# One decoder layer on one core: query and key loads of the prompt's heads on SyncE's queue, the samples' recurrence traced in two pieces

## The chip, the core and the metric

The kernel runs on one core of a Trainium2 chip. The metric is the device time of one execution in microseconds (us). Work on an engine is issued in the order of that engine's queue: PE (TensorE), DVE (VectorE), ACT (ScalarE), POOL (GpSimd) and SP (SyncE, which only issues transfers and waits). Sixteen DMA engines move the data of all queues.

## The reference

The kernel computes one layer for 1024 prompt tokens and, beside them, 8 sample sequences of 8 tokens each. The mixing part has two halves of 512 channels: a recurrent one (8 heads of 64 channels, a matrix state per head) and an attention one (8 heads, three dilated windows, a distance bias). Both feed one output projection, and a mixture of experts follows. The two parts that the change touches are these:

```python
def wkv_scan(s0, r, decay, k, v, kk, a):
    def step(s, inp):
        r_t, w_t, k_t, v_t, kk_t, a_t = inp
        s_kk = jnp.einsum('bhvk,bhk->bhv', s, kk_t)
        s = (s * w_t[:, :, None, :]
             - s_kk[..., None] * (kk_t * a_t)[:, :, None, :]
             + v_t[..., None] * k_t[:, :, None, :])
        return s, jnp.einsum('bhvk,bhk->bhv', s, r_t)
...
    scores = jnp.einsum('brnqhd,brnkhd->brnhqk', qb, kb) * (HEAD_DIM ** -0.5)
...
    o = jnp.einsum('brnhqk,brnkhd->brnqhd', e, vb) / jnp.swapaxes(den, -1, -2)[..., None]
```

The first is the recurrence; here it is the samples' that matters (8 sequences, 8 tokens, states from the cache). The second is the prompt's attention.

## The kernel before

Phase 1 normalizes the tokens, projects them (L264) and writes what later stages need to DRAM: among it the prompt's queries QP and keys KP, channel-major, each as an exact sum of two parts (a tensor of [2, 512, 1024]). Phase 2 runs the prompt's recurrence in chunks. Phase 3 is the attention, phases 4 to 6 are the output projection, the experts and the end.

**Attention of the prompt.** `phase3` (from L994) walks over pairs of heads; a pair has two heads, and a head has query tiles of 128 rows, ia to ib of 8. It is called twice: in the first call, while phase 2 still ends, heads 0 and 1 do tiles 0 to 4 (L936); in the second (L946) heads 0 and 1 do tiles 5 to 7, and pairs 1, 2 and 3 do all eight. For each tile PE multiplies queries with keys (L1040, two matmuls per 512 keys), DVE adds the bias and takes the maximum (L1043), ACT exponentiates (L1052), PE turns the result (L1063) and multiplies with the values (L1069), DVE scales (L1070).

**A head's operands** come from `head` (L963): keys `k` over both parts (128 rows: 64 channels of the high part, then 64 of the low part), queries `q` twice, once per part, each with its 64 rows given to both halves of the partitions, and the bias table. Each has two buffers, so a head's loads can start when the head two before it has done its last L1040. `head` is called for the head at work and for the next one. Its key and query loads are issued on POOL's queue (L971, L974), the bias on SP's (L976). Their source is a pattern written out by hand:

```python
        dup = lambda x, r, step, a, b: bass.AP(tensor=x.tensor, offset=x[0, r:r + 1, a:a + 1].offset, ap=[[step, 2], [NP, 64], [1, b - a]])
```

The outermost dimension of that source has two entries, and 64 rows lie in each. Another load of the kernel, on SP's queue, has a source of the same make: `At` in `solve` (L680), for the chunk systems of phase 2, 32 rows per load, with four entries outermost:

```python
                                  bass.AP(tensor=src.tensor, offset=src.offset, ap=[[0, 4], [1024, 8], [1, 1024]]))
```

**The samples' recurrence** is `phase2s` (L583), between the two calls of `phase3`. `prepA` and `prepB` make its operands, `solve_s` (L728) writes the 8 x 8 systems to DRAM (ABs, L620), reads them back one per partition (A8, L737), inverts them on DVE (L742, L744), writes them (XZ, L750) and reads them as TTs (L752). `sample2` (L792) then goes over four pairs of heads: it loads the cached states (s0s, L802), needs TTs in its matmul L820, and writes the new states (L844). `epilogue` (from L846) finishes the samples' rows. All PSUM of this part is one bank.

**Order.** The order of instructions on each engine is made at build time by a planner, which takes the traced order as priority and places an instruction when its operands and buffers are free by its own model of time. So where a piece is traced decides how early it stands in each queue. SP is in order too: behind an instruction that waits, all later loads of that queue wait. A hook of `phase3` runs just before a pair is traced: at pair 2 the samples' tiles are given up and w_out is loaded and split (`then`, L942). During pairs 1 and 2 twelve copies of the cache, 1016 KB each from DRAM to DRAM, are issued on SP (L281), each after an exponential.

Of the kernel before, what the change touches and what calls it, by code (L numbers as in the profile page):

```python
# [10 lines left out]
F32 = mybir.dt.float32  # L11
F32R = mybir.dt.float32r
F16 = mybir.dt.float16
# [8 lines left out]
NP = 1024  # L22
# [7 lines left out]
XB = 4      # tiles of x in flight  # L30
# [3 lines left out]
class K:  # L34
# [9 lines left out]
    def split(self, hi, lo, src, lo_eng=None, hi_eng=None):  # L44
        """hi + lo == src exactly; hi and lo carry float32r values."""
        nc = self.nc
        (hi_eng or nc.scalar).activation(hi, src, AF.Copy) if (hi_eng or nc.scalar) is nc.scalar else hi_eng.tensor_copy(hi, src)  # L47
        e = lo_eng or nc.vector
        return e.tensor_tensor(lo, src, hi.bitcast(F32), op=ALU.subtract)  # L49

    def bcast_row(self, vec, n):
        """DRAM vector of n values as [128, n], the same on each partition."""
        return bass.AP(tensor=vec.tensor, offset=vec.offset, ap=[[0, 128], [1, n]])

    def rstd(self, pool, ss, n, width, eps, scale, tag):
        """(ss*scale + eps)^-0.5 for a [n, width] tile."""
        nc = self.nc
        ms = pool.tile([128, width], F32, tag=tag + "m", name=tag + "m")
        nc.vector.tensor_scalar(ms[:n], ss, scale, eps, op0=ALU.mult, op1=ALU.add)
        r = pool.tile([128, width], F32, tag=tag + "r", name=tag + "r")  # L60
        nc.gpsimd.tensor_tensor(r[:n], ms[:n], self.mhalf[:n, :width], op=ALU.pow)  # L61
        return r
# [10 lines left out]
    def dram(self):  # L73
        d = self.es.enter_context(self.pool("dram", space=DRAM))
        self.dp = d
        t = lambda n, s, dt=F32: d.tile(s, dt, name=n)
        self.XV = t("XV", [4, 128, T])           # value, per pair of heads, channel-major
        self.ARd = t("ARd", [4, 128, 17, 128])   # per chunk: removal key | receptance, times the decay so far; last chunk: samples
        self.KB = t("KB", [4, 128, T])           # key over the decay so far
        self.BB = t("BB", [4, 128, T])           # removal key times a over the decay so far  # L80
        self.PC = t("PC", [4, 128, 24])          # decay over a chunk; 16 prompt chunks, 8 sequences
        self.BV = t("BV", [4, 128, T])           # bonus
        self.AA = t("AA", [4, 128, T])
        self.GG = t("GG", [4, 128, T])
        self.SS = t("SS", [T, 512])
        self.QP = t("QP", [2, 512, NP])          # prompt queries, channel-major, as an exact sum of two float32r parts
        self.KP = t("KP", [2, 512, NP])
        self.QT = t("QT", [4, 128, NS])
        self.KT = t("KT", [4, 128, NS])
        self.VS = t("VS", [NS, 512])  # L90
        self.KS = t("KS", [NS, 512])

# [1 line left out]
    def phase1(self):  # L94
        nc, tc, I, O = self.nc, self.tc, self.I, self.O
        with ExitStack() as es:
# [13 lines left out]
            # projection, 25 tiles of 128 columns, the lora tile first; the first two go along with the norm  # L110
# [33 lines left out]
            # last projected rows  # L144
# [7 lines left out]
    def vectors(self, c1):  # L152
        nc, I = self.nc, self.I
        nc.sync.dma_start(self.cst, I['cst'])
        # per-channel vectors, channel-major
# [23 lines left out]
        # mu * state_shift, [128, b, ct]  # L179
# [68 lines left out]
    def project(self, ct, out, chunks=range(3)):  # L248
        """columns 128 ct.. of the projection, channel-major; those of RWKV shifted by a token"""
# [28 lines left out]
    def copy(self, c, after):  # L278
        """Half of a sample's cache moves on, not before another instruction; the last rows come with the projection."""
# [33 lines left out]
    def lora(self, lora, lp):  # L313
        nc, I, vec, pm = self.nc, self.I, self.vec, self.pm1
        # contractions over 32 or 64 rows: the data's high and low parts stacked, the weights' parts in two passes
# [47 lines left out]
    def rwkv_ops(self, p, xr, xk, xv, ep):  # L363
        """per-token operands of a pair of heads: decay products within chunks, keys, bonus"""
# [7 lines left out]
        # decay so far within the chunk: before and after the token  # L372
# [17 lines left out]
        # removal key, normalized per head, negated  # L390
# [12 lines left out]
        # key  # L403
# [3 lines left out]
        # bonus  # L407
# [11 lines left out]
        # products with the decay  # L419
# [23 lines left out]
def host_consts():  # L443
    """Tables that depend on shapes alone."""
# [10 lines left out]
    # identity rows for a quarter of the columns: column 4c + d on partitions with (p // 8) % 4 == d  # L455
# [5 lines left out]
class K2(K):  # L461
# [17 lines left out]
    def pools2c(self, es):  # L479
        """tiles that stay over the RWKV stage and the samples' part of it"""  # L480
        nc = self.nc
        self.c2 = c2 = es.enter_context(self.pool("c2", side="right"))
        # zero-padded block-diagonal operands; the padding is written once
# [27 lines left out]
    def pools2a(self, es):  # L511
        """the first of pools2, opened while the projection still runs"""
# [28 lines left out]
    def phase2a(self):  # L541
        """the first chunks' systems, which the projection hides"""
# [40 lines left out]
    def phase2s(self):  # L583
        y = self.e2.tile([128, 512], F32, tag="y", name="y")
        G = self.prepA('s')
        self.prepB('s', G)
        self.solve_s(G)
        self.sample2(G, y)
        self.epilogue(NP, y, 64)

    def pair_load(self, dst, src, t0, nck):
        """[pair, channel, token] into the block-diagonal [channel, chunk, pair, (head, token)]"""
# [5 lines left out]
    def prepA(self, u):  # L598
        """what the chunk systems and the states' first products need; two chunks, or the samples"""
# [71 lines left out]
    def solve(self, u, G):  # L671
        """(I - A)^-1 of each 64 x 64 chunk system: 32-row halves by forward substitution, joined by products.
        Partition (head of the pair, half, column mod 4, chunk and pair)."""
# [19 lines left out]
    def join(self, u, G):  # L693
        nc, sv, X = self.nc, self.sv, G['X']
        TT = G['TT'] = self.TT[u % 2]
        R1 = sv.tile([128, 8, 32], F32, tag="R1", name="R1")     # rows: [t, column / 4, (column mod 4, system)]
        RT = sv.tile([128, 8, 32], F32, tag="RT", name="RT")     # transposed: [column, system, t]
# [3 lines left out]
        # diagonal halves; systems of pairs 0, 1 on rows 0..63, of pairs 2, 3 on rows 64..127  # L701
# [26 lines left out]
    def solve_s(self, G):  # L728
        """inverse of the 8 x 8 systems, one per partition (pair, head, sequence)"""
# [62 lines left out]
    def sample2(self, G, y):  # L792
# [4 lines left out]
        for p in range(4):  # L797
            # states, rows (sequence parity, v), then turned to [(head, k), (sequence, v)]
# [28 lines left out]
            for j, (src, lhs) in enumerate(((G['Vt'][:, 0, p, :], G['Kt']), (u, G['Bt']))):  # L827
                # rows spread over their sequence
# [69 lines left out]
class K3(K2):  # L898
# [3 lines left out]
    def attn_out(self, pool, X, at, n, i0, gat, tags=("asq", "an", "ao"), bufs=1, w=512):  # L902
        """rmsnorm of [n, 512] mixed heads, then channel-major into MX[4:8]."""
# [19 lines left out]
    def phase123(self):  # L923
# [5 lines left out]
        with ExitStack() as ea:  # L929
# [16 lines left out]
            self.phase3([(0, 5, 8), (1, 0, 8), (2, 0, 8), (3, 0, 8)], 3, (3, 2, 1, 1), {AHEAD: then})  # L946
# [16 lines left out]
    def head(self, h, ia, ib):  # L963
        """a head's operands for query tiles ia..ib"""
# [4 lines left out]
        # keys: high over low part; queries: either part twice  # L969
        k = self.qk.tile([128, NP], F32R, tag="k", name="k3")  # L970
        nc.gpsimd.dma_start(k[:, :w], dup(self.KP, h * 64, 512 * NP, 0, w))  # L971
        q = self.qk.tile([128, 2, NP], F32R, tag="q", name="q3")
        for a in range(2):
            nc.gpsimd.dma_start(q[:, a, 128 * ia:w], dup(self.QP[a:a + 1], h * 64, 0, 128 * ia, w))  # L974
# [4 lines left out]
    def samples_out(self, pool, X, n, w):  # L979
        """the samples' heads, from rows per head to rows per token"""  # L980
# [13 lines left out]
    def phase3(self, pairs, depth, banks, hooks={}):  # L994
        nc, tc, I, O = self.nc, self.tc, self.I, self.O
        gat, at = self.gat, self.at
        with ExitStack() as es:
# [5 lines left out]
            else:       # stays for the following phases  # L1003
# [154 lines left out]
ORD = (8, 0, 1, 2, 3, 4, 5, 6, 7)     # of the token tiles in phase 4, and of their routing tables  # L1158
# [16 lines left out]
class K4(K3):  # L1175
# [8 lines left out]
    def ahead(self):  # L1184
        """w_out, loaded and split while the attention still runs"""
# [34 lines left out]
    def pst(self, tag):  # L1220
        """a bank of PSUM, from the rings of the attention"""
# [8 lines left out]
    def hold(self, d, after):  # L1230
        """a load that waits for an instruction"""
# [3 lines left out]
    def load_w(self, j, after=(None, None), part=(0, 1)):  # L1235
        """block j: -2, -1 w_out; 0..31 the experts' gate | up; 32, 33 w_ple_gate"""
# [13 lines left out]
    def split_w(self, j, q, eng=None, after=None):  # L1250
        """quarter q of block j"""
# [8 lines left out]
    def load_d(self, j, after=None):  # L1260
        """block j: 0..31 the experts' down; 32 w_ple; 33 p of the prompt"""
# [16 lines left out]
    def mm3(self, p, a, b, k0, k1, kn, c=slice(0, 512)):  # L1278
        """p += a^T b over chunks k0..k1 of kn, in three float32r passes"""
# [11 lines left out]
    def phase4_(self, p4):  # L1291
# [19 lines left out]
        ones = p4.tile([128, 128], F16, name="ones")      # counts and token numbers are exact in float16  # L1311
# [43 lines left out]
        def logits(i, last=False):  # L1355
            """of the router; the norm's gain is in its weights, its scale comes last"""
# [18 lines left out]
        def route(i0, nb):  # L1375
            """experts, weights and slots of nb token tiles"""
# [4 lines left out]
            def first_max(src, w, iota, tag):  # L1381
                """max over w columns and the one-hot of its first place"""
# [18 lines left out]
            # one-hots of the two experts; rank within the expert, in token order  # L1401
# [16 lines left out]
            # token of each slot: one-hot of the rank times one-hot of the expert times the token's number  # L1418
# [10 lines left out]
            # slots, and weights: softmax of the two, times the group's  # L1429
# [12 lines left out]
            # rows past the capacity: their weight moves to the overflow table  # L1442
# [38 lines left out]
    def embed(self):  # L1481
        """p @ w_ple, kept in DRAM; token tiles in pairs"""
# [142 lines left out]
    def overflow(self, e):  # L1625
        """Tokens past an expert's capacity: that expert on all tokens, weighted by the overflow table."""
# [66 lines left out]
    def phase6(self):  # L1693
# [63 lines left out]
        def finish(i, j):  # L1757
            """mix and out of the last tile, half by half"""
# [109 lines left out]
```

## Time and profile before

| what | value |
|---|---|
| median of 3 runs | 1621.02 us |
| the three runs | 1618.59, 1627.01, 1621.02 us |
| span of the profiled execution, first to last instruction | 1623.8 us |
| PE busy | 1398.6 us (86%) |
| DVE, ACT, POOL busy | 960.8, 722.2, 549.1 us |
| bytes moved by DMA | 350.02 MB, mean 216 GB/s |

The profiled execution has no time of its own beside its span; the span lies within the three runs' times and 2.8 us above their median. Busy times of engines overlap, and an engine that others wait for shows it as their idle time. The attention of the prompt, with the samples' recurrence in it, lies between about 680 us and 940 us of the span.

### The profile page before, as it was taken

What the parts mean: (1) busy time and instruction counts of PE and PEld (TensorE: products, weight loads), DVE (VectorE), ACT (ScalarE), POOL (GpSimd) and SP (SyncE); (2) the same over time, 40 slices, a digit from 0 to 9 for tenths busy, and PEclk for the clock granted to TensorE, in tenths of its full rate; (3) what the DMA queues carried; (4) which work ended last, traced back from release to release, by engine and by line L of the source; (5) the groups of instructions that cost most, each with busy time, mean ns of one, the idle gap of its engine ahead of it and who ended that gap; (6) DMA issues with size and microseconds to landing.
All of it is one profiled execution on the core that took longest, in us unless ns stands there. A gap on an engine that the chain in (4) does not pass through costs nothing. (4 is left out here: it accounts for less than half of the span.)

```text
span 1623.8 us, 24626 instructions
## 1 busy us (share of the span) xinstructions
PE 1398.6 (86%) x9017; PEld 1159.6 (71%) x9018; DVE 960.8 (59%) x2121; ACT 722.2 (44%) x1304; POOL 549.1 (34%) x427
## 2 busy tenths in 40 slices
PE   4999999999889889973988999948988788797996
PEld 4888999999667767762867787836765455565884
DVE  7524663551476857343656534459876678686664
ACT  5535453231334435341444633327765566674332
POOL 8004651001122222431223513126675454454230
PEclk9999999999979898986999998979999899899998
DMA  6156558895774753366676566579999799996551
GB/s 200 53 177 188 153 164 284 301 348 179 200 219 138 190 162 115 90 138 156 202 209 187 157 212 213 188 246 319 340 364 336 241 309 319 319 348 220 189 183 65
DMA packets 306158, 350.02 MB, mean 216 GB/s; under 512 B 105757, under 2 KB 249951, under 8 KB 305504
## 3 DMA queue, kind: packets, MB, share of 16 engines
q1 hardware_dynamic: 261424, 287.46, 56.4%
q0 software_dynamic: 39712, 43.76, 9.7%
q10 hardware_dynamic: 4896, 17.17, 2.8%
q8 instruction: 73, 1.20, 0.3%
q14 instruction: 53, 0.43, 0.1%
HBM read 277.45 MB, written 104.33 MB: 235 GB/s over the span
## 5 line engine op out<-in xcount | busy, mean ns | idle before, releaser
L49 POOL TENSOR_TENSOR dl<-draw,dh 128x1024 fp32r<-128x1024 f32 x66 | 175.3, 2678 | 98.8 <-ACT dh L47 98.7
L264 PE MATMUL pj<-hT_hi,wh 128*128 128x384 f32 (+1 forms) x600 | 198.9, 333 | 4.7 <-DVE lora L272 2.7
L264 PE MATMUL pj<-hT_hi,wl 128*128 128x384 f32 (+1 forms) x600 | 198.6, 331 | 0.0
L264 PE MATMUL pj<-hT_lo,wh 128*128 128x384 f32 (+1 forms) x600 | 198.0, 330 | 0.0
L264 PEld LDWEIGHTS pj<-hT_hi,wh 128*128 128x128 f32 x600 | 113.4, 190 | 6.6 <-DVE lora L272 3.0
L264 PEld LDWEIGHTS pj<-hT_hi,wl 128*128 128x128 f32 x600 | 113.6, 189 | 2.4 <-issue 2.2
L264 PEld LDWEIGHTS pj<-hT_lo,wh 128*128 128x128 f32 x600 | 113.9, 190 | 0.6 <-issue 0.2
L47 ACT ACTIVATE dh<-draw 128x1024 fp32r<-128x1024 f32 x66 | 66.3, 1052 | 70.2 <-PE p4y L1283 41.2
L688 DVE TENSOR_TENSOR ftmp<-At,X 128x60 f32<-128x60 f32 (+24 forms) x248 | 59.3, 251 | 44.7 <-DMA At<-ABd 26.9
L1040 PE MATMUL pS<-k,q 128*128 128x512 f32 (+2 forms) x192 | 56.3, 401 | 33.6 <-DMA q<-QP 32.2
L1524 POOL DMA_INDIRECT x<-HN,idx x32 | 51.3, 1604 | 94.0 <-PE p4t L1534 37.8
L1069 PEld LDWEIGHTS po<-v,pt 128*128 128x128 f32 x576 | 74.2, 197 | 10.7 <-issue 2.4
L1069 PE MATMUL po<-v,pt 128*128 128x128 f32 x576 | 79.8, 284 | 1.4 <-ACT pt L1067 1.1
L1052 ACT ACTIVATE s<-s,nm 128x128 f32<-128x128 f32 (+7 forms) x64 | 49.4, 772 | 61.8 <-DVE X L744 21.3
L767 POOL TENSOR_TENSOR s<-S,pc 128x512 f32<-128x512 f32 x16 | 16.9, 1053 | 162.6 <-PE pj L264 69.9
L690 DVE TENSOR_TENSOR X<-X,ftmp 128x60 f32<-128x60 f32 (+24 forms) x248 | 59.0, 250 | 4.5
L49 DVE TENSOR_TENSOR wl<-w,wh 128x1024 fp32r<-128x1024 f32 x25 | 35.0, 1400 | 44.7 <-ACT wh L47 43.9
L1043 DVE CUSTOM_DVE_ANT_0 s<-pS,bias 128x512 f32<-128x512 f32 (+2 forms) x96 | 50.9, 552 | 17.7 <-PE pxt L1063 13.2
L1040 PEld LDWEIGHTS pS<-k,q 128*128 128x128 f32 x192 | 32.7, 208 | 39.9 <-issue 21.8
L1283 PE MATMUL p4y<-dh,hl 128*96 128x512 f32 x128 | 52.4, 409 | 5.5 <-DVE hl L49 5.5
L1067 ACT ACTIVATE pt<-pxt 128x512 f32<-128x512 f32 (+3 forms) x64 | 32.6, 512 | 54.7 <-PE pxt L1063 41.8
L1283 PE MATMUL p4y<-dh,hh 128*96 128x512 f32 x128 | 48.1, 416 | 5.5 <-ACT hh L47 5.3
(653 smaller groups left out, 3874.9 us busy)
## 6 DMA issues: line engine op xcount, KB each, us to landing
wraw<-in_w_gate_dram SPq DMA_DIRECT2D x64, 512.0 KB
wraw<-in_w_up_dram SPq DMA_DIRECT2D x64, 512.0 KB
draw<-in_w_down_dram SPq DMA_DIRECT2D x32, 1024.0 KB
out_dram<-in_cache_k_win_dram SPq DMA_DIRECT2D x16, 1016.0 KB
out_dram<-in_cache_v_win_dram SPq DMA_DIRECT2D x16, 1016.0 KB
w<-in_w_in_dram SPq DMA_DIRECT2D x25, 512.0 KB
kc<-in_cache_k_win_dram SPq DMA_DIRECT2D x48, 256.0 KB
vc<-in_cache_v_win_dram SPq DMA_DIRECT2D x48, 256.0 KB
```

The lines of the kernel that those rows point to most:

```text
L47: (hi_eng or nc.scalar).activation(hi, src, AF.Copy) if (hi_eng or nc.scalar) is nc.scalar else hi_eng.tensor_copy(hi, src)
L49: return e.tensor_tensor(lo, src, hi.bitcast(F32), op=ALU.subtract)
L264: nc.tensor.matmul(p[:, :nn], a[:, k, :], b[:, k, n0:n0 + nn], start=(m == 0), stop=(m == 23))
L688: nc.vector.tensor_tensor(o, At[:, t, t + 1:32][:, :, None].to_broadcast([128, m, c]), X[:, t, None, 0:c].to_broadcast([128, m, c]), op=AL ...
L690: nc.vector.tensor_tensor(X[:, t + 1:32, 0:c], X[:, t + 1:32, 0:c], o, op=ALU.add)
L1040: nc.tensor.matmul(ps[:, :n], q[:, a, i * 128:(i + 1) * 128], k[:, c0:c0 + n], start=(a == 0), stop=(a == 1))
L1043: nc.vector.tensor_tensor_reduce(s[:, c0:c0 + n], ps[:, :n], bias[:, bo:bo + n], 1.0, -3e38, ALU.add, ALU.max, m)
L1052: ex = nc.scalar.activation(s[:, :nb * 128], s[:, :nb * 128], AF.Exp, bias=nm, accum_out=den)
L1067: nc.scalar.activation(pt[:, b0:b0 + m, :], px[:, :m, :], AF.Copy)
L1069: nc.tensor.matmul(po, pt[:, b, :], v[:, b, :], start=(b == 0), stop=(b == nb - 1))
L1283: self.nc.tensor.matmul(p, a[x][:, k, :], w, start=(k == 0 and q == 0), stop=(k == kn - 1 and q == 2))
L1524: nc.gpsimd.indirect_dma_start(out=X[e][:n], out_offset=None, in_=self.HN, in_offset=bass.IndirectOffsetOnAxis(ap=self.idx[:, e:e + 1], ax ...
```

## The change

The key and query loads of `head` are issued by SP, with the destination seen as plain float32; the data moved, the buffers and the patterns stay. `phase2s` keeps the preparation and the inverse of the samples' systems; `sample2` and `epilogue` move into a new function, `phase2t`, which the second `phase3` call traces just before pair 1. Comments are taken out elsewhere, which changes nothing that runs.

```diff
     def phase2s(self):
-        y = self.e2.tile([128, 512], F32, tag="y", name="y")
-        G = self.prepA('s')
+        G = self.G['s'] = self.prepA('s')
         self.prepB('s', G)
         self.solve_s(G)
-        self.sample2(G, y)
+
+    def phase2t(self):
+        y = self.e2.tile([128, 512], F32, tag="y", name="y")
+        self.sample2(self.G['s'], y)
         self.epilogue(NP, y, 64)
...
-            self.phase3([(0, 5, 8), (1, 0, 8), (2, 0, 8), (3, 0, 8)], 3, (3, 2, 1, 1), {AHEAD: then})
+            self.phase3([(0, 5, 8), (1, 0, 8), (2, 0, 8), (3, 0, 8)], 3, (3, 2, 1, 1), {1: self.phase2t, AHEAD: then})
...
         k = self.qk.tile([128, NP], F32R, tag="k", name="k3")
-        nc.gpsimd.dma_start(k[:, :w], dup(self.KP, h * 64, 512 * NP, 0, w))
+        nc.sync.dma_start(k[:, :w].bitcast(F32), dup(self.KP, h * 64, 512 * NP, 0, w))
         q = self.qk.tile([128, 2, NP], F32R, tag="q", name="q3")
         for a in range(2):
-            nc.gpsimd.dma_start(q[:, a, 128 * ia:w], dup(self.QP[a:a + 1], h * 64, 0, 128 * ia, w))
+            nc.sync.dma_start(q[:, a, 128 * ia:w].bitcast(F32), dup(self.QP[a:a + 1], h * 64, 0, 128 * ia, w))
```

## Rows read from the trace of the kernel before

**Rows 1.** The page, its first line.

```profile
span 1623.8 us, 24626 instructions
```

**Rows 2.** Windows: length, busy us per engine, granted clock, DMA share, GB/s; attention stage.

```profile
680.00:890.00 210.00, 157.91 (x1027) 131.14 (x1028) 108.23 (x421) 77.80 (x180) 62.00 (x69) 0.87 0.68 179
```

**Rows 3.** Waits, 670 to 940 us: us in total, times, longest us.

```profile
PE pS L1040 <- DMA q<-QP: 32.2, 6, 12.9
PEld pS L1040 <- DMA k<-KP: 7.2, 1, 7.2
PE pas L817 <- DVE X L744: 14.4, 1, 14.4
DVE t L742 <- DMA s0s<-in_state_wkv_dram: 14.1, 1, 14.1
POOL k L971 <- PE pS L1040: 21.8, 7, 5.6
```

**Rows 4.** PE's timeline: start us, us, instruction, idle before it and its releaser.

```profile
745.86 0.77 PE L817 MATMUL pas<-vt,LAK 128*128 128x128 f32 x2 [14.44 <-DVE X L744]
...
771.60 0.44 PE L1040 MATMUL pS<-k,q 128*128 128x128 f32 x1 [12.86 <-DMA q<-QP]
...
819.04 0.66 PE L1040 MATMUL pS<-k,q 128*128 128x128 f32 x2 [6.93 <-DMA q<-QP]
```

**Rows 5.** Groups of instructions by line, 670 to 940 us: busy us, mean ns, idle.

```profile
L974 POOL DMA_DIRECT2D q<-QP x20 | 15.9, 810 | 0.0
...
L971 POOL DMA_DIRECT2D k<-KP x10 | 8.6, 862 | 21.8 <-PE pS L1040 21.8
```

**Rows 6.** All instructions on tile q: ns min/median/max, first and last start, landing.

```profile
L1040 PE MATMUL pS<-k,q x192: 221/395/796, 695.0 to 914.9; 128*128 128x512 f32 x96, 128*128 128x128 f32 x32, 128*128 128x256 f32 x32, 128*128 128x384 f32 x32
...
DMA to landing us min/median/max: 12.6/18.6/25.8
```

**Rows 7.** DMA issues of the whole span: count, size of one, median us to landing.

```profile
q<-QP POOLq DMA_DIRECT2D x12, 512.0 KB, 19.2
...
k<-KP POOLq DMA_DIRECT2D x8, 512.0 KB, 17.3
...
q<-QP POOLq DMA_DIRECT2D x4, 320.0 KB, 12.9
...
q<-QP POOLq DMA_DIRECT2D x4, 192.0 KB, 17.5
...
k<-KP POOLq DMA_DIRECT2D x2, 320.0 KB, 13.1
```

**Rows 8.** POOL's timeline: first head's loads and the last head's.

```profile
681.19 1.09 POOL L971 DMA_DIRECT2D k<-KP  x1
...
866.51 1.59 POOL L974 DMA_DIRECT2D q<-QP  x2
```

**Rows 9.** SP's timeline, At loads of phase 2, and DVE's first use of the second set.

```profile
519.49 2.74 SPq L680 DMA_DIRECT2D At<-ABd  x4
...
594.29 2.83 SPq L680 DMA_DIRECT2D At<-ABd  x4
...
603.46 0.19 DVE L688 TENSOR_TENSOR ftmp<-At,X 128x31 f32<-128x31 f32 x1 [9.99 <-DMA At<-ABd]
```

**Rows 10.** Windows, columns as in group 2: At, At under traffic, head loads.

```profile
522.10:523.60 1.50, 1.50 (x16) 1.50 (x15) 0.00 (x0) 1.50 (x4) 1.02 (x1) 1.00 0.25 104
...
599.10:601.20 2.10, 0.00 (x0) 0.00 (x0) 0.00 (x0) 0.42 (x1) 0.10 (x1) 1.00 0.98 282
...
736.60:738.40 1.80, 0.00 (x0) 0.00 (x0) 0.00 (x0) 0.00 (x0) 0.00 (x0) 0.50 0.16 50
757.50:759.90 2.40, 1.24 (x9) 0.80 (x8) 1.79 (x6) 0.86 (x2) 0.56 (x1) 1.00 0.46 148
```

**Rows 11.** SP's timeline, the samples' loads: start us, us, line, transfer, count.

```profile
727.32 7.01 SPq L802 DMA_DIRECT2D s0s<-in_state_wkv_dram  x5
734.37 5.15 SPq L737 DMA_DIRECT2D A<-ABs  x4
```

## The prediction

> **What bounds the kernel now.** I read the page first: the profiled execution spans 1623.8 us [rows 1], with PE the busiest engine. PE is not busy everywhere, so I went to the stage that the change touches, 680 to 890 us. There PE is busy 157.9 of 210 us, the DMA engines 0.68 of the time at 179 GB/s [rows 2]: 52 us of PE's idle time lie here. The waits say whose: 32.2 us until the queries of a head land, in six waits, and 14.4 us behind the inverse of the samples' systems; the weight loads' 7.2 us for the keys overlap the first [rows 3]. PE's timeline gives the places: 14.4 us before the samples' matmul at 745.9, 12.9 us before the first head of pair 1, 6.9 us before the first of pair 2 [rows 4]. So this stage is bound by transfers that come late, not by PE's work. The question for a change of queue is how long a head's loads take on the new one.
>
> **How many engines a load runs on.** This decides the sum. A head of pairs 1 to 3 brings three loads of 512 KB, which land some 17 to 19 us after their issue [rows 6, 7]. With the loads of one head in flight and little else, 757.5 to 759.9, the share is 0.46 of 16 engines, about seven, at 148 GB/s. Near the end of the loads issued before, with all compute engines idle, it is 0.16, between two and three engines, at 50 GB/s, which I read as one load left [rows 10]. So I take two engines per load on POOL's queue and different pairs for the three loads of a head: the source leads with a dimension of two.
>
> SP's queue has the same make of load: At, whose source leads with four. Four of them are issued from 519.49 on; from 522.1 to 523.6, with all four issued, the share is 0.25, four engines, at 104 GB/s [rows 9, 10], 26 GB/s each. If each took other engines, the share would be near 1. So on SP's queue a load gets as many engines as its leading dimension has entries, and **all such loads get the same ones, one behind the other**. The heads' source leads with two: on SP I expect two engines for all ten heads, at 52 GB/s together.
>
> The Trainium skill says the same of the choice: "DMA: Bandwidth & Descriptors", section "Why a DMA increments its semaphore by 16 and not by 1", has the engine count as the largest number up to 16 that divides the slowest dimension of both sides, the lowest-numbered engines on SP's queue, and consecutive engines from a moving cursor on POOL's. By that rule the sum is the one below; the At row (0.25 with four loads issued) agrees. That the two engines are the same pair for every head is not shown by a head's own load here, only by At.
>
> **The change part by part.**
>
> *Issue on POOL goes.* 30 instructions: 20 x 0.81 and 10 x 0.86 us, 24.5 us of POOL, and 21.8 us in which POOL waited for the last query matmul of an older head [rows 3, 5]. POOL is busy 62 of 210 us here [rows 2]: it hides both. Nothing.
>
> *Issue on SP comes.* 30 more instructions, 0.6 to 0.7 us each by the At loads (2.74 us for four [rows 9]), about 20 us over 210 us, hidden. The waits for an older head's matmuls now hold SP: behind them stand the bias tables, the values, the cache copies and the samples' small transfers; DVE waits for the bias, PE for the values. Alone that is bounded by POOL's 21.8 us above and zero below. I take zero, since the loads themselves will be later than what waits behind them.
>
> *The loads' time.* 12 + 8 loads of 512 KB, 4 + 2 of 320 KB and 4 of 192 KB [rows 7] make 12,928 KB, 13.24 MB. At 52 GB/s that is **255 us**. Against it stand about 205 us from the first issue (681.2) to the landing of the last (its second query load is issued at about 867.3, plus the median 18.6 us, 886) [rows 6, 8]. So two engines alone already take 50 us more than the stage has.
>
> *The other traffic on the same two engines.* 179 GB/s over 210 us are 37.6 MB [rows 2]; less the heads' 13.2, 24.4 MB remain, of which two of sixteen engines carry a sixteenth each: 1.52 MB, at 26 GB/s **59 us**. Bounds: 0, if all of it came after the last head's load, to 59. I take 59: copies, bias and values of the earlier heads are issued before it, on the same queue.
>
> *Traffic on the fourteen others* slows the two. The At loads issued from 594.29 on, 512 KB, were first used at 603.46, with a share of 0.98 at 282 GB/s around them [rows 9, 10]: 57 GB/s for four engines, 28.6 for two. Between 52 and 28.6 I take 52, as PE will wait and little else run. At 282 GB/s the other 24.4 MB last 87 us; were all of that at the slower rate, the heads would move 2.5 instead of 4.5 MB in it, **38 us** more. This goes into the range.
>
> *The recurrence in two pieces.* Before, five state loads took 7.0 us of SP just ahead of the systems' loads (A), of which SP had issued four by 739.5 us; DVE stood 14.1 us for them and PE 14.4 us [rows 3, 11]. (DVE's wait is put down to a state load, but the instruction reads A.) With the states traced a pair later, A comes sooner and this wait would go. But A spreads over several engines, the heads' two among them: ABs, A, XZ and TTs, each waiting for the one before, can each stand behind a head's load. A head's last three tiles bring 512 + 2 x 192 KB, 17.6 us at 52 GB/s. DVE, which waits in order, holds the tiles behind it, and the head after next is requested later. Bounds: 0 to two such loads, 35 us. I take **10 us** of idle time on the two engines, because mostly another head's load is already queued. The four pairs' own work moves into waits that PE then has anyway: nothing. Its cover would go if the loads were fast; then it competes with pairs 1 to 3 as now.
>
> **The sum.** 681 + 255 + 59 + 10 = 1005 us for the last landing, against 886: **119 us later**. What follows (the last head's eight tiles, the projection) starts from there as before. 1623.8 + 119 = 1742.8; the span stands 2.8 us above the median of the runs, so **1740 us**.
>
> **The rivals.**
>
> *Fast loads.* SP's loads spread over all engines. A 512 KB load at 282 GB/s [rows 10] takes 1.9 us, a head's three 5.6 us, and the waits on queries and on the samples go: 32.2 + 14.4 = 46.6 us at most [rows 3]. DVE and ACT come next, so I take 40: 1581 us. For it: most loads of this queue run on all engines. Against it: At, by its leading four. It decides if the share with only head loads in flight is near 1. Chance 0.07.
>
> *Only the issuer changes.* Each load keeps its two own engines and its 17 to 19 us; the query waits stay, and the samples' 14.4 us go or turn up at the next head: 1607 to 1621 us. The trace is against it: At shows SP's loads queueing on the same engines, unlike 0.46 for a head on POOL's [rows 10]. Chance 0.04, half of it within 0.5%. The Trainium skill speaks for this one ("DMA: Bandwidth & Descriptors", "Issuing engines are not separate DMA queues": issuing elsewhere saves only the sequencer's time). By that rule the time is the 1607 to 1621 us above; the At row speaks against it for loads with a short leading dimension.
>
> *SP's order.* The loads keep their time, and the 21.8 us of waits now hold bias and values [rows 3]: 1621 + 22 = 1643 us. Chance 0.02: the waits are 5.6 us at most, and a tile's bias is asked for early.
>
> **How the numbers follow.** The two-engine case has 0.87. Its low end is 681 + 255 with none of the other terms, 50 us later, 1671, rounded to 1665; its high end 1740 + 38 + 25 (the rest of the samples' bound), rounded to 1800. Some 0.07 of this case may lie outside, so the range holds about 0.8; the faster rivals are left out. A measurement of this kernel can tell 0.5%, 8 us, from no change. Faster by more: 0.07 + 0.02 = 0.09; within: 0.02; slower: 0.87 + 0.02 = 0.89.
>
> **What would show it.** Right: in a stretch with only head loads in flight the share is near 0.125 at about 50 GB/s; the waits for keys and queries grow from 32 us to over 120 us, on nearly every head; the interval from one head's first query matmul to the next's grows towards 30 us (1.57 MB at 52 GB/s) in pairs 1 to 3; the last query matmul, at 914.9 us before [rows 6], comes past 1020; after it the kernel runs as before. Samples: A lands behind a head's load, not at once. Wrong: a share of 0.3 or more with head loads alone, or waits that shrink, would refute the two engines; a last landing before 950 us would mean that the other traffic lies behind, not among, the loads.

## The result, and the profile after

| | before | after |
|---|---|---|
| median of 4 runs on one chip | 1624.01 us (1618.59 to 1630.40) | 1742.99 us (1738.21 to 1746.27) |
| ratio, 95% interval | | 1.0734 [1.0693, 1.0775] |
| span of the profiled execution | 1623.8 us | 1736.5 us |
| first and last query-key matmul | 695.0, 914.9 us | 686.6, 1048.0 us |
| from the last of these to the end | 708.9 us | 688.5 us |

The kernel is 7.3% slower, as forecast (1740 us). The last two lines of the table say already that the way there is not quite the forecast one: the attention ends 133 us later, and what follows is 20 us shorter. Lines of the changed kernel that stand behind L585 have numbers higher by two.

Windows of the changed kernel, columns as in [rows 2]: the stretch of [rows 2], and two of 20 us.

```profile
680.00:890.00 210.00, 102.11 (x581) 83.88 (x578) 62.23 (x248) 47.33 (x109) 20.51 (x22) 0.72 0.31 100
860.00:880.00 20.00, 16.18 (x117) 13.86 (x115) 10.12 (x42) 8.78 (x20) 2.08 (x2) 1.00 0.13 51
900.00:920.00 20.00, 20.00 (x134) 17.66 (x133) 12.20 (x48) 8.99 (x21) 5.20 (x5) 0.90 0.15 56
```

Read the last two numbers first. The stage moves 100 GB/s where it moved 179 [rows 2], and for 20 us on end the share is 0.13 at 51 GB/s: that is the share of two of sixteen engines, while a head's three loads are wanted. PE is busy 102 us instead of 158, and the granted clock of the stage falls with it, from 0.87 to 0.72. On POOL's queue a head in flight had 0.46 and 148 GB/s [rows 10].

Waits of the changed kernel, 670 to 1060 us, as in [rows 3].

```profile
PE pS L1042 <- DMA q<-QP: 105.8, 14, 14.2
PEld pS L1042 <- DMA q<-QP: 68.1, 8, 10.4
...
PE pxt L916 <- DVE an L913: 21.2, 1, 21.2
DVE wrt L1196 <- DMA gfc<-in_norm_ffn_dram: 19.5, 1, 19.5
...
ACT asq L910 <- DMA ats<-ATS: 18.1, 1, 18.1
PE pS L1042 <- DVE m L1045: 16.7, 3, 16.0
DVE t L744 <- DMA A<-ABs: 16.3, 1, 16.3
```

PE's wait for queries grew from 32.2 us in 6 places [rows 3] to 105.8 in 14, and its weight loads (PEld) wait another 68.1. The wait on the samples' systems is still there, 16.3 us on DVE against 14.1, now put down to A itself. Two are new: the samples' attention rows (ats, 18.1 us on ACT, seen by PE as 21.2), and gfc, a small table of the next phase, for which DVE stands 19.5 us (0.5 before).

PE's timeline of the changed kernel, the long waits of the last heads, as in [rows 4].

```profile
883.64 0.45 PE L1042 MATMUL pS<-k,q 128*128 128x128 f32 x1 [7.46 <-DMA q<-QP]
...
893.65 0.47 PE L1042 MATMUL pS<-k,q 128*128 128x128 f32 x1 [9.56 <-DMA q<-QP]
...
923.91 0.30 PE L1042 MATMUL pS<-k,q 128*128 128x128 f32 x1 [2.46 <-DMA q<-QP]
...
934.32 0.47 PE L1042 MATMUL pS<-k,q 128*128 128x128 f32 x1 [10.11 <-DMA q<-QP]
...
965.72 0.45 PE L1042 MATMUL pS<-k,q 128*128 128x128 f32 x1 [5.56 <-DMA q<-QP]
...
976.17 0.47 PE L1042 MATMUL pS<-k,q 128*128 128x128 f32 x1 [10.01 <-DMA q<-QP]
...
1008.22 3.36 PE L1071 MATMUL po<-v,pt 128*128 128x128 f32 x14 [19.29 <-DVE at L1072]
...
1030.56 0.48 PE L1042 MATMUL pS<-k,q 128*128 128x128 f32 x1 [10.12 <-DMA q<-QP]
```

The three heads shown in pairs of lines have two waits each, for the first and for the second of their query loads, and the second ends 10.0, 10.4 and 10.5 us after the first: 512 KB in 10.0 us are 52 GB/s. The loads run one behind the other on two engines, as the prediction had it. From head to head it is 40.7 and 41.9 us, not the 30 that a head's 1.57 MB take alone: other traffic goes over the same two engines in between.

SP's timeline of the changed kernel, around one head and the last head's loads (start us, us, line, transfer, count), and all its issues of q (ns min/median/max, first and last start).

```profile
896.87 0.56 SPq L973 DMA_DIRECT2D k<-KP  x1
897.48 11.88 SPq L976 DMA_DIRECT2D q<-QP  x2
909.46 9.66 SPq L978 DMA_DIRECT2D bias<-in_abase_dram  x1
...
981.61 3.01 SPq L976 DMA_DIRECT2D q<-QP  x1
984.73 7.59 SPq L1192 DMA_DIRECT2D wrt<-in_w_group_dram  x1
992.42 9.69 SPq L872 DMA_DIRECT2D MX<-o  x1
...
1006.67 0.98 SPq L1249 DMA_DIRECT2D wraw<-in_w_out_dram  x2
...
1008.40 0.49 SPq L976 DMA_DIRECT2D q<-QP  x1
...
L976 SPq DMA_DIRECT2D q<-QP x20: 494/3926/12007, 671.6 to 1008.4; - x20
```

Two issues take 11.9 us together and the one behind them 9.7; over all twenty of q the median is 3.9 and the longest 12.0, where the forecast had 0.6 to 0.7. So SP itself stands while the heads' loads are queued, and what stands behind them in its order comes late: gfc, for which DVE stands from 988.0 to 1007.5 us and PE from 988.9 to 1008.2, and the last head's second query load, 26.8 us after its first and behind two loads of w_out.

### The profile page after: what moved, and what is told of

Read it like the earlier page. It is cut to its first block, busy times and chain, and to the rows that moved or that the text cites. A ratio compares the mean times of both kernels' runs of the same rounds, so it can differ in the third digit from the quotient of the medians.

```text
span 1736.5 us, 24599 instructions
## 1 busy us (share of the span) xinstructions
PE 1409.7 (81%) x9017; PEld 1169.4 (67%) x9018; DVE 951.5 (55%) x2121; ACT 721.8 (42%) x1304; POOL 520.9 (30%) x397
## 5 line engine op out<-in xcount | busy, mean ns | idle before, releaser
L1042 PE MATMUL pS<-k,q 128*128 128x512 f32 (+2 forms) x192 | 61.6, 419 | 124.0 <-DMA q<-QP 105.8
L1042 PEld LDWEIGHTS pS<-k,q 128*128 128x128 f32 x192 | 34.6, 221 | 132.9 <-DMA q<-QP 68.1
L1071 PE MATMUL po<-v,pt 128*128 128x128 f32 x576 | 88.2, 304 | 22.6 <-DVE at L1072 19.7
L1071 PEld LDWEIGHTS po<-v,pt 128*128 128x128 f32 x576 | 81.9, 215 | 33.8 <-DVE at L1072 20.0
L1072 DVE TENSOR_SCALAR at<-po,rd 128x64 f32<-128x64 f32 x64 | 18.0, 282 | 107.0 <-PE po L1071 106.9
L1526 POOL DMA_INDIRECT x<-HN,idx x32 | 50.2, 1570 | 68.5 <-PE p4t L1536 32.2
```

What stands on the lines that cost most here:

```text
L1042: nc.tensor.matmul(ps[:, :n], q[:, a, i * 128:(i + 1) * 128], k[:, c0:c0 + n], start=(a == 0), stop=(a == 1))
L1071: nc.tensor.matmul(po, pt[:, b, :], v[:, b, :], start=(b == 0), stop=(b == nb - 1))
L1526: nc.gpsimd.indirect_dma_start(out=X[e][:n], out_offset=None, in_=self.HN, in_offset=bass.IndirectOffsetOnAxis(ap=self.idx[:, e:e + 1], ax ...
```

## The experiments

Ratios are to the kernel before, run on the same chip. "End" is the start of the last query-key matmul, "rest" the span less that. Both are read from one profiled execution, which can lie some us off its kernel's median: that of `sp_lead8` is 10 us above, that of the changed kernel 5 us below.

| kernel | median us | ratio, 95% interval | end | rest |
|---|---|---|---|---|
| queue_only | 1761.56 | 1.0909 [1.0879, 1.0939] | 1056.2 | 697.3 |
| recurrence_only | 1616.27 | 1.0003 [0.9977, 1.0029] | 919.9 | 701.2 |
| sp_lead4 | 1649.31 | 1.0183 [1.0110, 1.0257] | 937.3 | 708.6 |
| sp_lead8 | 1611.71 | 0.9951 [0.9920, 0.9982] | 904.3 | 715.3 |
| sp_rows64 | 1557.36 | 0.9636 [0.9597, 0.9675] | 866.4 | 688.1 |
| pool_rows64 | 1574.10 | 0.9727 [0.9687, 0.9767] | 867.4 | 706.5 |
| no_copies | 1715.51 | 1.0574 [1.0494, 1.0654] | 1023.7 | 691.4 |
| act_keys | 1744.28 | 1.0785 [1.0751, 1.0820] | 1047.9 | 698.3 |
| sp_rows64_one | 1569.14 | 0.9688 [0.9617, 0.9760] | 861.8 | 704.7 |
| pool_rows64_two | 1574.38 | 0.9747 [0.9722, 0.9772] | 864.1 | 705.6 |
| sp_rows64_again | 1552.19 | 0.9603 [0.9578, 0.9629] | 866.1 | 689.0 |
| pool_rows64_again | 1570.83 | 0.9726 [0.9702, 0.9750] | 867.5 | 707.9 |

**The two halves of the change.** `queue_only` moves the loads and keeps the recurrence in one piece:

```diff
             self.phase2s()
+            self.phase2t()
...
-            self.phase3([(0, 5, 8), ...], 3, (3, 2, 1, 1), {1: self.phase2t, AHEAD: then})
+            self.phase3([(0, 5, 8), ...], 3, (3, 2, 1, 1), {AHEAD: then})
```

> The loads on SyncE's queue, the samples' recurrence in one piece as before. Two engines for all head loads: 1735 to 1765 us, since the split of the recurrence is worth 20 us at most either way; the query and key waits of PE and of its weight loads stay above 120 us. Rival, that the slowdown comes from the recurrence being traced a pair later: about 1624 us. Rival, that both halves share it: near 1680 us.

Measured: 1761.56 us, 9.1% slower, within what was expected. The queue alone is the whole loss, and more than that; with the loads on SP the second edit takes 1.75 points back (1.0909 against 1.0734, on two chips).

`recurrence_only` keeps the loads on POOL and splits the recurrence:

```diff
-        nc.sync.dma_start(k[:, :w].bitcast(F32), dup(self.KP, h * 64, 512 * NP, 0, w))
+        nc.gpsimd.dma_start(k[:, :w], dup(self.KP, h * 64, 512 * NP, 0, w))
...
-            nc.sync.dma_start(q[:, a, 128 * ia:w].bitcast(F32), dup(self.QP[a:a + 1], h * 64, 0, 128 * ia, w))
+            nc.gpsimd.dma_start(q[:, a, 128 * ia:w], dup(self.QP[a:a + 1], h * 64, 0, 128 * ia, w))
```

> The loads back on GpSimd's queue, the samples' recurrence in two pieces. Two engines for all head loads on SyncE: this is not slower than before, 1605 to 1625 us; the 14.4 us before the samples' first matmul go or shrink, the query waits stay at 25 to 40 us. Rival, the recurrence a pair later is what costs: 1680 us or more.

Measured: no change, 1.0003. The waits of this kernel, 670 to 940 us, and its SP timeline:

```profile
PE pS L1042 <- DMA q<-QP: 35.3, 7, 14.8
...
PE pas L819 <- DVE X L746: 14.6, 1, 14.6
DVE t L744 <- DMA s0s<-in_state_wkv_dram: 14.2, 1, 14.2
```

```profile
724.89 7.36 SPq L804 DMA_DIRECT2D s0s<-in_state_wkv_dram  x5
732.30 5.83 SPq L739 DMA_DIRECT2D A<-ABs  x4
```

The wait on the samples' systems stands as it did (14.6 us against 14.4, [rows 3]), and five state loads still stand right ahead of A on SP, 7.36 us against 7.01 [rows 11]. The planner places a load when its buffer is free by its model, which is the likely reason that tracing the user later did not move it. That the wait "would go" was wrong.

**How many engines a load gets.** `sp_rows64` swaps the two leading dimensions of the heads' source in the changed kernel; the same rows land on other partitions, alike in keys and queries. `pool_rows64` does the same to the kernel before.

```diff
-        ... ap=[[step, 2], [NP, 64], [1, b - a]])
+        ... ap=[[NP, 64], [step, 2], [1, b - a]])
```

> The changed kernel with the two leading dimensions of the heads' source swapped, so that it leads with 64 rows and two entries lie inside; keys and queries get the same order of rows, so the products are the same sums. Same queue, same number of loads, same bytes. Two engines by the leading dimension: now sixteen engines, a head's 1.57 MB in 6 to 10 us, the query and key waits below 15 us, the time 1575 to 1605 us. Rival, SyncE's order (its waits for older heads hold everything behind them): over 1700 us, as changed. Rival, the loads are slow for their 4 KB rows or for reading the same bytes twice: over 1700 us.

> The kernel of before with the same swap of the two leading dimensions, loads on GpSimd's queue. If six engines per head is what made its loads land after 17 to 19 us, they land in under 10 us, the 32 us of query waits fall below 12, and the time is 1590 to 1610 us. Rival, GpSimd's queue is slow in itself (its own work per row): landings stay near 17 us and the time at 1624 us.

Measured: 1557.36 and 1574.10 us, both faster than the kernel before and than was expected. The window of [rows 2] in `sp_rows64`, then the waits on its tile q:

```profile
680.00:890.00 210.00, 196.71 (x1321) 164.32 (x1322) 133.56 (x516) 110.97 (x245) 60.57 (x55) 0.98 0.66 215
```

```profile
L976 SPq DMA_DIRECT2D q<-QP x20: 550/604/1297, 675.9 to 838.4; - x20
...
  DMA q<-QP: 0.8, 2
```

One line is changed, and in the same 210 us PE does 1321 matmul instructions instead of the changed kernel's 581; the wait for queries is 0.8 us, and SP's issue of q is back at 0.6 us in the median. In `pool_rows64` the time to landing, as in [rows 6], fell from a median of 18.6 us to 6.7:

```profile
DMA to landing us min/median/max: 3.7/6.7/9.9
```

`sp_lead4` and `sp_lead8` give the values in between: each load is cut in two of 64 rows, with a source that leads with n = 4 or 8.

```diff
+        rows = lambda x, r, a, b: bass.AP(..., ap=[[NP, n], [n * NP, 64 // n], [1, b - a]])
...
-        nc.sync.dma_start(k[:, :w].bitcast(F32), dup(self.KP, h * 64, 512 * NP, 0, w))
+        for g in range(2):
+            nc.sync.dma_start(k[64 * g:64 * g + 64, :w].bitcast(F32), rows(self.KP[g:g + 1], h * 64, 0, w))
...
+            for g in range(2):
+                nc.sync.dma_start(q[64 * g:64 * g + 64, a, 128 * ia:w].bitcast(F32), rows(self.QP[a:a + 1], h * 64, 128 * ia, w))
```

> The changed kernel, but each load of a head is cut in two of 64 rows (256 KB) whose source leads with four; the rows are permuted alike in keys and queries. Theory (on SP's queue a load runs on as many engines as its leading dimension has entries, always the same ones): four engines, 104 GB/s; 13.24 MB take 127 us, the other traffic on the same four engines 59 us, together 186 us, about what the stage has (681 to 866). So most of the loss goes: 1580 to 1640 us, and in stretches with only head loads a share near 0.25 at about 104 GB/s. Rival (the count of loads, or SP's time to issue them, is what costs): 60 issues instead of 30, so not faster than the changed kernel's 1743 us.

> As sp_lead4, with a source that leads with eight. Theory: eight engines, 208 GB/s; 13.24 MB take 64 us, the others' 59 us lie beside them, so the loads are no longer what the stage waits for: 1555 to 1595 us, near sp_rows64's 1557. Rival (what helped sp_rows64 was another order of the rows in memory, not the number of engines): the same time as sp_lead4, within 10 us.

Measured: 1649.31 and 1611.71 us, 9 and 17 us above what was expected. With a leading 2, 4, 8 and 64 the attention ends at 1048.0, 937.3, 904.3 and 866.4 us, and all waits on queries come to 173.9, 22.2, 8.8 and 0.8 us: each step up in engines brings the stage in, though the loads are twice as many at 4 and 8. Both rivals fall: the count of loads is not what costs, and the order of rows alone would have put 4 and 8 at one time. Stretches with little but heads' loads in flight show the engines themselves (columns as in [rows 2]), first of `sp_lead4`, then two of `sp_lead8`:

```profile
768.00:774.00 6.00, 2.11 (x7) 1.29 (x7) 0.51 (x2) 0.00 (x0) 0.00 (x0) 0.56 0.26 105
...
798.00:801.00 3.00, 3.00 (x28) 2.98 (x27) 2.40 (x10) 0.41 (x2) 1.04 (x1) 1.00 0.51 205
771.00:777.00 6.00, 6.00 (x46) 5.17 (x45) 2.39 (x9) 2.04 (x6) 1.04 (x1) 1.00 0.52 126
```

A share of 0.26 is four engines and 0.51 eight, as many as the source leads with. But in the last stretch eight engines move 126 GB/s instead of 205; no run here shows why. The times were missed because of this and because more than the queries waits. DVE's wait on the samples' systems (L744) is 16.3, 10.0, 5.7 and 1.5 us at 2, 4, 8 and 64. The rest is also 20 and 27 us longer in these two than in the changed kernel (of the 27, up to 10 may be the profiled execution's); the order of the instructions there is another one, to which the last group of experiments comes back.

**Whose traffic shares the pair.** `no_copies` is the changed kernel without the twelve cache copies of pairs 1 and 2, so those rows of the caches are not written.

```diff
-                        if p in (1, 2) and nb in (4, 6, 8):
-                            self.copy(ncopy, ex)
-                            ncopy += 1
```

> The changed kernel without the twelve copies of the samples' caches that are issued in pairs 1 and 2 (rows of k_s and v_s stay unwritten); the heads' loads stay on two engines. Theory (the other traffic on the same two engines stands in line with the loads): a copy is about 1 MB, 65 KB for each of 16 engines, 2.5 us at 26 GB/s, so twelve of them take 30 us of the two engines' time: 1743 - 30, 1700 to 1722 us. Rival (the other traffic fits in gaps of the two engines, the loss is the loads alone): 1735 to 1750 us.

Measured: 1715.51 us, and the attention ends 24.3 us sooner. The loads themselves, from the first issue (675.2) to the last landing (just before 1003.2), take 328.0 us instead of 359.5, 31.5 less. Twelve copies were worth 30 us of the pair's time by their bytes: the term is there at its size.

`act_keys` is the changed kernel with the keys' loads issued by ScalarE.

```diff
-        nc.sync.dma_start(k[:, :w].bitcast(F32), dup(self.KP, h * 64, 512 * NP, 0, w))
+        nc.scalar.dma_start(k[:, :w].bitcast(F32), dup(self.KP, h * 64, 512 * NP, 0, w))
```

> The changed kernel, but the keys' loads (a third of the heads' bytes) are issued by ScalarE, whose queue is another one, done in hardware as SyncE's is. Theory (such queues put a load with a leading dimension of two on the same two engines whichever engine issues it): with only head loads in flight the share stays near 0.13 at about 52 GB/s, and the time is the changed kernel's, 1735 to 1775 us (the upper end for ScalarE's own waits at the keys' buffers). Rival (each queue has its own pair): the share reaches 0.25 at about 104 GB/s, the queries alone are 170 us on their pair plus 59 us of other traffic, last landing near 910: 1630 to 1670 us.

Measured: 1744.28 us, the end at 1047.9 against 1048.0. Windows of this kernel, columns as in [rows 2]:

```profile
830.00:835.00 5.00, 0.00 (x0) 0.00 (x0) 0.00 (x0) 0.00 (x0) 0.00 (x0) 0.50 0.13 52
865.00:880.00 15.00, 10.28 (x76) 8.69 (x75) 7.58 (x31) 5.69 (x14) 2.12 (x3) 0.96 0.13 52
885.00:890.00 5.00, 0.00 (x0) 0.00 (x0) 0.00 (x0) 0.00 (x0) 0.00 (x0) 0.50 0.94 308
900.00:905.00 5.00, 0.00 (x0) 0.00 (x0) 0.00 (x0) 0.00 (x0) 0.00 (x0) 0.50 0.13 53
```

The first of these windows by queue, SP's (q1) and ScalarE's (q10): packets, MB, share of 16 engines.

```profile
q1 hardware_dynamic: 32, 0.13, 6.4%
q10 hardware_dynamic: 32, 0.13, 6.4%
```

Both queues move a load here, half each, and together they have 0.13 at 52 GB/s with PE idle; in between the bias and the copies burst through nearly all engines at 308. ScalarE's queue has the same two engines as SP's for a load of this make. That is what no row of before could show.

**Queue or recurrence, once the loads are wide.** `sp_rows64_one` is `sp_rows64` with the recurrence in one piece (the diff of `queue_only`); `pool_rows64_two` is `recurrence_only` with the swap of `pool_rows64`; the two others are repeated beside it.

> sp_rows64 with the samples' recurrence traced in one piece, so that it differs from pool_rows64 by the issuing queue alone and from sp_rows64 by the recurrence alone. If the 17 us between pool_rows64 (1574) and sp_rows64 (1557) come from the queue: 1550 to 1565 us. If from the split of the recurrence: 1567 to 1582 us.

> pool_rows64 with the samples' recurrence in two pieces, so that it differs from sp_rows64 by the issuing queue alone. Theory (the queue's wait was gone in pool_rows64, and the split only moves work off the pair in which the samples stand in the way): some 8 us faster than pool_rows64, 1560 to 1570 us, and 3 to 8 us slower than sp_rows64. Rival (with the loads on GpSimd's queue the split does nothing, as in recurrence_only): pool_rows64's time within 4 us.

> The kernel of sp_rows64 once more, beside pool_rows64_again and pool_rows64_two on one chip: 1550 to 1565 us, ratio to the kernel before 0.960 to 0.967.

> The kernel of pool_rows64 once more on the same chip as sp_rows64_again: ratio to the kernel before 0.969 to 0.977. If the queue alone makes no difference once all sixteen engines carry a load, then what separates the two is the split of the recurrence, and pool_rows64_two stands at sp_rows64_again.

Measured: `sp_rows64` keeps its lead on one chip (0.9603 against 0.9726). `pool_rows64_two` was expected some 8 us below `pool_rows64` and stands at it (0.9747): on POOL's queue the split does nothing, here too. As `pool_rows64_two` and `sp_rows64` differ by the queue alone, SP's queue is worth 1.4 points where the recurrence is split, though the source leads with 64 in both. `sp_rows64_one` (1569.14 us, in the band named for the split) lies between and its interval reaches towards both, so what the queue is worth without the split is not settled. But the lead does not arise in the attention, which ends at 861.8 to 867.5 us in all four. The rest is 688 to 689 us in `sp_rows64` and 705 to 708 in the others. Windows of `sp_rows64`, from the end of its attention:

```profile
866.00:955.00 89.00, 88.60 (x510) 72.95 (x508) 40.31 (x102) 34.94 (x64) 23.40 (x30) 1.00 0.60 191
955.00:1028.00 73.00, 52.33 (x309) 44.09 (x310) 41.08 (x130) 19.11 (x29) 13.97 (x17) 0.87 0.72 243
1028.00:1378.00 350.00, 303.06 (x1404) 208.21 (x1405) 265.14 (x298) 228.15 (x329) 198.06 (x86) 0.95 0.99 322
```

The same stretches of `pool_rows64_two`, up to the last matmul that turns an expert's tokens:

```profile
864.00:958.00 94.00, 89.61 (x517) 73.72 (x515) 39.96 (x107) 38.54 (x71) 30.47 (x33) 1.00 0.61 195
958.00:1034.60 76.60, 56.96 (x308) 47.96 (x308) 40.81 (x130) 18.99 (x29) 14.24 (x17) 0.82 0.64 223
1034.60:1390.00 355.40, 305.06 (x1408) 210.79 (x1409) 265.70 (x299) 228.24 (x330) 195.84 (x86) 0.93 0.97 319
```

Five, four and five us: the projection, its end with the routing, and the experts each take a little less, in stages whose code is the same. What does differ is the order of the instructions that the planner made there. From the end of the attention PE's matmuls (2915 of them, by operation and tile) come in one and the same order in `sp_rows64`, its repetition and the changed kernel, and their rests are 688.1, 689.0 and 688.5 us. In another order (2924) they come in the kernel before, in `recurrence_only` and in all three `pool_rows64` kernels, with rests of 701.2 to 708.9 us. So the rest goes with the order, not with the number of engines that the heads' loads had. That the order alone is the cause was not tried.

`sp_rows64` is the fastest version: 3.6 to 4.0% below the kernel before, and 10.5% below the changed kernel by spans (1554.5 against 1736.5).

## Why the prediction was right

**Two engines, the same pair for all heads: right.** 0.13 at 51 GB/s for 20 us on end, 10.0 to 10.5 us per 512 KB load, and, in `act_keys`, the same pair even from another queue. The step that the prediction could only take from the At loads [rows 10] is now shown by heads' own loads, and 4 and 8 engines by `sp_lead4` and `sp_lead8`. Of the signs named, the share, the waits on queries (173.9 us, 120 forecast) and the last query matmul (1048.0 us, past 1020) came; from one head to the next it is 41 us rather than 30, and the kernel does not run on as before. The Trainium skill ("DMA: Bandwidth & Descriptors", section "Why a DMA increments its semaphore by 16 and not by 1") gives the count of engines and says that the hardware queues take the lowest-numbered ones; the counts and `act_keys` agree with it, though the profile shows shares and not the engines' numbers. The rival taken from its section "Issuing engines are not separate DMA queues" fell: for a load that gets two engines, POOL's queue or SP's is 9.1%. For the wide load it holds as far as the attention goes (866.4 and 867.4 us).

**The sum, term by term.** The loads ran from 671.0 us (their first issue; 681 was taken from [rows 8]) to just before 1030.6: 359 us, where 255 + 59 + 10 = 324 had been summed. The last landing came 25 us later than the 1005 predicted. The window of all loads:

```profile
671.00:1030.00 359.00, 189.07 (x1132) 155.18 (x1130) 114.06 (x445) 87.20 (x196) 49.18 (x46) 0.73 0.34 114
```

- Heads' bytes, 255 us: the rate of 52 GB/s held.
- Other traffic on the pair, 59 us: this is the term that was mis-sized. By bytes (40.9 MB, less the heads' 13.2, an eighth of the rest at 52 GB/s) it would be 67 us. But a share of 0.34 over 359 us is 1953 us of engine time; less the heads' 2 x 255, a sixteenth of the rest is 90 us for each engine. That is an estimate, which takes the other traffic as evenly spread. It is more than by bytes because this traffic moves slower than 26 GB/s per engine: 308 GB/s at a share of 0.94 (`act_keys`) are 20. Right in kind (`no_copies`), 31 us short.
- Idle time of the pair, 10 us: in 2-us windows from 671 to 1031 the share is below 0.115 in ten of them, worth 10 us. Right in size; the reason given for it was half wrong (`recurrence_only`). What was feared, the samples' transfers behind the heads', is there, 18.1 us for ats and 16.3 us for A, but as waits of the compute engines and not as idle time of the pair.
- Traffic on the fourteen other engines, taken as 0 with a bound of 38: 359 less 255, 90 and 10 leaves 4 us. By this estimate nothing of size is left for it.

**SP's issue, costed at nothing: wrong.** "About 20 us over 210 us, hidden" used 0.6 to 0.7 us each. With the pair's queue full an issue of q takes 3.9 us in the median and up to 12.0, and then gfc holds DVE 19.5 us and the last query load waits. In the middle of the stage the loads cover this, at its end nothing does; its price is likely part of the 25 us by which the last landing came late, and no run here parts it from the rest.

**"Starts from there as before": wrong by 20 us.** The rest fell from 708.9 to 688.5 us (of these 20, up to 5 may be the changed kernel's profiled execution's). The changed kernel has the shorter order of the two told of above, a side effect of the edit that no step had. So 133 us later and 20 us shorter made 113 us by spans, against 119 forecast. The sign and the mechanism were read from the profile; that the total came within 3 us of the median is in part two errors that cancelled.

**Rivals.** "Fast loads" is what the kernel becomes with the swap. It ended at 1557 where 1581 had been worked out: the attention ends 48.5 us sooner than before (866.4 against 914.9), close to the 46.6 us of waits that bounded it, and the rest is 20.8 us shorter, which no step had. "SP's order" was real as an addition, not as a replacement.

## What to carry to other kernels

Before a load is moved to another queue, look at how many engines it gets: the share of the DMA engines in a stretch where only that load is in flight (0.13 is two of sixteen), and whether several of them in flight raise it. A source that leads with a short dimension gets few engines; swapping it with a longer one cost nothing here, as keys and queries take the new order of rows alike, and was worth 2.7% on POOL's queue and 10.5% on SP's. When a kernel's order is planned by a program, compare the untouched stages too, since an edit can move them by as much as the effect that is looked for.

## What the runs showed of the hardware that was not expected

- With the loads before it queued on two engines, an issue of q on SP takes 3.9 us in the median and up to 12.0, and the issue of the bias behind them up to 9.7. In `sp_rows64`, on the same queue, an issue of q takes 0.6 us in the median.
- A share of busy engines is not a rate: eight engines at 0.51 and 0.52 moved 205 and 126 GB/s in two stretches of `sp_lead8`.
- ScalarE's queue does not add engines for such a load: 52 GB/s for both queues together.
- On POOL's queue the swap cut the median time to landing from 18.6 to 6.7 us, and the stage then ends within 1 us of SP's.
